# A hybrid layer on one core: a third pair of weight buffers while the mixers run, and the low parts of 27 weight units made by ScalarE and an accumulating DMA

## The chip, the cores and the metric

The kernel runs on one core of one Trainium2 chip. The time is the device time of one execution in microseconds (us). Each engine of the core works through its own list of instructions in order: TensorE (PE; its weight loads are listed as PEld), VectorE (DVE), ScalarE (ACT), GpSimd (POOL) and SyncE (SP). SP and POOL, and now and then ACT, also issue DMAs. A change of time of about 1% is what a measurement of this kernel can tell from no change.

## The reference, cut to what matters

One layer works on x of 512 x 1024 in float32. Its input is normalised, multiplied by one wide weight, and split among four sequence mixers (gated delta rule, RG-LRU, S5, RWKV-7) and four gates; the branches are merged, projected, and followed by an MLP and a last norm:

```python
h = _rmsnorm(x, norm1_g)
proj = h @ w_in                                   # 1024 x 6920: mixers' columns, then 4 x 1024 gate columns
p_gdn, p_lru, p_s5, p_rwkv, p_gate = _split(proj, (GDN_COLS, LRU_COLS, S5_COLS, RWKV_COLS, GATE_COLS))
ys = (_gdn_mixer(p_gdn, ...), _rglru_mixer(p_lru, ...), _s5_mixer(p_s5, ...), _rwkv7_mixer(p_rwkv, ...))
for i in range(N_BRANCH):
    term = sigmoid(gate_logits[:, :, i]) * (ys[i] @ w_branch[i])
    merged = term if merged is None else merged + term
x = x + merged @ w_out
x = x + square(relu(_rmsnorm(x, norm2_g) @ mlp_w1)) @ mlp_w2
return _rmsnorm(x, final_norm_g)
```

## The kernel before

Every large product is done in split precision. A weight comes in blocks of 128 x 1024 float32 (512 KB), called units here; there are 134 loads of them. For a unit u, `load` (L307) lets SP fetch the block into a buffer of the ring `raw` (four buffers, tags raw0 to raw3, taken in turn). `unit` (L316) then makes two parts of it: the high part `hi` is the block rounded to TensorE's short float32 form, written by ScalarE as a plain copy (`act`, L117), and the low part `lo` is what is left, block minus `hi`, written by VectorE (`tt`, L120). `gemm` (L337) issues for each of eight slices k three matmuls of 128 x 512: `hi` with the high part of x, `hi` with its low part, and `lo` with its high part, 24 in all. So the third matmul of a unit is the first that reads `lo`.

The pairs of `hi` and `lo` are two (DEEP = 2, tags hi0/lo0 and hi1/lo1) up to the MLP. The MLP takes two more tiles (`third`), so that three pairs take turns there; it also sums some of its weights with DMAs that add to what lies in the buffer (`accum_op=ADD`, issued by GpSimd, L330 and L332). Eighteen of these write a tile of the region c, six a raw buffer.

The work before the MLP is cut into steps named in PLAN: the first norm, the projection of each mixer's columns (two columns of weight units at a time), the mixers' own recurrences with many small matmuls, and the gates and branches between them. A scheduler turns the program into one fixed list for each engine; `priority(100 * u - 30000)` in `unit` places each unit's load and split ahead of most other work, as far as its buffers are free. So which instruction stands behind which on an engine is settled before the kernel runs, and an instruction that waits holds up all that stands behind it on that engine. The units 3 to 29 that are spoken of below are those of the last RWKV columns, S5, the delta rule, RG-LRU, and the first gate columns; unit 29 is done about a quarter of the way through the span.

Some names in the lists: acc is a unit's result in PSUM, zpr, t1pr and z3pr belong to one mixer's small products, glu to S5's last step, bkT and ktT to transposes for the recurrences, scrr and scu to scratch in HBM, c0, c1a, c1b, c2, c3 to regions of SBUF that many small tiles share (printed as c, c1a, c1b in the trace).

Of the kernel before, what the change touches and what calls it, by code (L numbers as in the profile page):

```python
# [9 lines left out]
F = mybir.dt.float32  # L10
R = mybir.dt.float32r
ACT = mybir.ActivationFunctionType
# [3 lines left out]
ADD, SUB, MUL, MAX = ALU.add, ALU.subtract, ALU.mult, ALU.max  # L16
# [40 lines left out]
GRAN = 32  # L57
DEEP = 2
NRAW = 4

GROUPS = ((8, True), (8, True), (8, True), (8, False))
REST = 21568
# [38 lines left out]
def trunk(ctx, tc, order, xT, wall, w8, prm, big, cst, gfr, out):  # L101
    nc = tc.nc
    V, A, G, P = nc.vector, nc.scalar, nc.gpsimd, nc.tensor

    const = ctx.enter_context(tc.tile_pool(name="const", bufs=1))
    wp = ctx.enter_context(tc.tile_pool(name="wp", bufs=1))
# [9 lines left out]
    def act(o, i, f, scale=1.0, bias=0.0):  # L116
        A.activation(out=o, in_=i, func=f, scale=scale, bias=bias)  # L117

    def tt(e, o, a, b, op):
        e.tensor_tensor(out=o, in0=a, in1=b, op=op)  # L120
# [72 lines left out]
    @contextmanager  # L193
    def priority(n):
        old = tc.cur_priority
        tc.cur_priority = n
        yield
        tc.cur_priority = old
# [32 lines left out]
    def v3(t, a):  # L231
        return t.rearrange("p (a b) -> p a b", a=a)
# [69 lines left out]
    third = []  # L302

    def place(key):
        if key not in order:
            order.append(key)
        return order.index(key)  # L307

    def load(key):
        n = count["raw"]  # L310
        count["raw"] += 1
        raw = wp.tile([128, 1024], F, tag=f"raw{n % NRAW}", name=f"raw{n}")
        nc.sync.dma_start(out=raw, in_=wall[place(key)])
        return raw

    def unit(key, more=None, chain=None):  # L316

        u = count["u"]
        count["u"] += 1
        with priority(100 * u - (30000 if u else 50000)):  # L320
            k = u % (DEEP + len(third) // 2)
            if k < DEEP:
                hi, lo = (wp.tile([128, 1024], R, tag=f"{e}{k}", name=f"{e}{u}") for e in ("hi", "lo"))
            else:
                hi, lo = third
            if chain is None:
                raw = load(key)
            else:
                raw = chain
                (G if more is None else nc.sync).dma_start(out=raw, in_=wall[place(key)], **({"accum_op": ADD} if more is None else {}))  # L330
            if more is not None:
                G.dma_start(out=raw, in_=wall[place(more)], accum_op=ADD)  # L332
            act(hi, raw, ACT.Copy)
            tt(V, lo, raw, hi.bitcast(F), SUB)
        return v3(hi, 8), v3(lo, 8)

    def gemm(o, w, rh, rl, nk=8, k0=0, first=True, last=True):  # L337
# [75 lines left out]
    def proj(col):  # L413

        o = pa("acc")
        gemm(o, unit(("in", col)), xgh, xgl)
        return o
# [964 lines left out]
    def branch(i, hf):  # L1382

        if i not in ysp:
            ysp[i] = split_y(ys[i], str(i))
        y = ysp[i]
        yh, yl = v3(y[0], 2), v3(y[1], 2)
        wh, wl = (t.rearrange("p (k m) c -> p k m c", k=2) for t in unit(("br", i, hf)))
        for mi, gt in enumerate(gates[i, hf]):
            m = 4 * hf + mi  # L1390
            o = pa("bacc")
            gemm(o, (wh[:, :, mi, :], wl[:, :, mi, :]), yh, yl, nk=2)
            if m not in mg:
                mg[m] = t2("mg", where=("c3",))
                tt(V, mg[m], o, gt, MUL)
            else:
                tt(V, gt, o, gt, MUL)
                tt(V, mg[m], mg[m], gt, ADD)
            fr(gt)
        gates.pop((i, hf))  # L1400
        if not any(k[0] == i for k in gates) and done_[i]:
            fr(*y)
        done_[i] = True
# [3 lines left out]
    def merge():  # L1407
        mh_, ml_ = t16("mh", R), t16("ml", R)
        mh, ml = v3(mh_, 8), v3(ml_, 8)
        for m in range(8):  # L1410
            act(mh[:, m, :], mg[m], ACT.Copy)
            tt(V, ml[:, m, :], mg[m], mh[:, m, :].bitcast(F), SUB)
            fr(mg[m])
        for m in range(8):
            o = pa("oacc")
            gemm(o, unit(("out", m)), mh, ml)
            tt(V, x2[m], o, x2[m], ADD)
        fr(mh_, ml_)
# [401 lines left out]
```

## Time and profile before

| | |
|---|---|
| median of three runs (lowest, highest) | 888.55 us (887.16, 894.03) |
| the profiled execution: time, span | 892.66 us, 890.9 us |
| PE busy, share of the span | 869.9 us, 98% |
| DVE, ACT, POOL busy | 549.8, 422.7, 24.2 us |
| mean granted clock of TensorE | 0.985 |

The profiled execution is 4.11 us above the median of the three. An engine's busy time counts its own instructions, not the issue of DMAs. Rows of groups give a line, an engine, an operation, the tile written and the tiles read, the count, the busy time and the mean of one, and then the idle time before them and what ended it. A row of a timeline gives the start, the duration, the engine (SPq for the issue of a DMA by SP), the line and the tiles. A row of windows gives a stretch of the span, the busy time of PE, PEld, DVE, ACT and POOL with their counts of instructions, the granted clock of TensorE, the busy share of the sixteen DMA engines and what they moved.

### The profile page before, as it was taken

Reading aid. Unit: us, or ns where it says so; the run is one execution under the profiler, and the core shown is the slowest. Engines: PE = TensorE matmul, PEld = TensorE weight load, DVE = VectorE, ACT = ScalarE, POOL = GpSimd, SP = SyncE. Lnnn points to the kernel's source line nnn. Section 1 sums busy time; section 2 is a strip of 40 time slices with the busy share of each in tenths; the row PEclk is TensorE's granted clock in tenths of the full one; section 3 lists DMA queues with packets and bytes.
Section 4 is the critical chain, followed back from the end, with each engine's and each line's share of the span. In section 5 each row is a group of like instructions: output and inputs, shape, how many; then the busy total and the mean of one; then the engine's idle time right before and its main releaser. Section 6 shows DMA issues by size and latency. Waiting matters only on the chain.

```text
span 890.9 us, 12990 instructions
## 1 busy us (share of the span) xinstructions
PE 869.9 (98%) x5175; PEld 696.8 (78%) x5175; DVE 549.8 (62%) x967; ACT 422.7 (47%) x584; POOL 24.2 (3%) x37
## 2 busy tenths in 40 slices
PE   8999999989899999999999999999999999999996
PEld 6777777768677777777888878888888888888885
DVE  6899796983666245845566554346436554868543
ACT  8735548845422243242633343756545443644533
POOL 1000000000000000000000000000100010010000
PEclk9999999998999889999999999999999999999999
DMA  8433344464355543243322223554775867563302
GB/s 292 134 117 103 113 118 93 108 175 112 119 177 149 155 121 94 95 128 109 106 96 95 94 94 121 187 143 166 145 207 146 259 161 196 162 146 113 118 24 95
DMA packets 79292, 119.96 MB, mean 135 GB/s; under 512 B 42544, under 2 KB 49392, under 8 KB 79216
## 3 DMA queue, kind: packets, MB, share of 16 engines
q1 hardware_dynamic: 51968, 100.40, 35.2%
q0 software_dynamic: 3456, 12.58, 8.3%
q10 hardware_dynamic: 23808, 6.16, 3.2%
q8 instruction: 40, 0.66, 0.3%
q14 instruction: 20, 0.16, 0.1%
HBM read 103.79 MB, written 13.17 MB: 131 GB/s over the span
## 4 chain that ended last, share of the span: by engine, by line
PE 85%; DVE 6%; ACT 3%; DMA 3%; issue 1%; ACTq 1%; SPq 0%; DVEq 0%
PE acc L114 28%; PE facc L114 20%; PE dacc L114 17%; PE oacc L114 5%; PE bacc L114 5%; DVE c L120 2%; PE oT L114 2%; DMA c1a<-gscr 1%; ACT c L117 1%; PE s L114 1%; DVE lo L120 1%; DVE c L129 1%; PE glu L114 1%; ACT L117 1%; PE gj L114 0%
## 5 line engine op out<-in xcount | busy, mean ns | idle before, releaser
L114 PE MATMUL acc<-c,hi 128*128 128x512 f32 x864 | 279.5, 401 | 4.4 <-DVE c L129 2.5
L117 ACT ACTIVATE hi<-raw 128x1024 fp32r<-128x1024 f32 x113 | 119.5, 1058 | 235.4 <-PE facc L114 73.6
L120 DVE TENSOR_TENSOR lo<-raw,hi 128x1024 fp32r<-128x1024 f32 x113 | 138.0, 1222 | 114.7 <-ACT hi L117 111.7
L114 PEld LDWEIGHTS acc<-c,hi 128*128 128x128 f32 x864 | 162.3, 190 | 45.3 <-DVE c L129 5.0
L114 PE MATMUL acc<-c,lo 128*128 128x512 f32 x432 | 174.9, 406 | 1.2 <-DVE lo L120 1.2
L114 PE MATMUL facc<-c,hi 128*128 128x512 f32 x336 | 103.4, 389 | 0.0
L114 PEld LDWEIGHTS acc<-c,lo 128*128 128x128 f32 x432 | 82.3, 191 | 21.1 <-DVE lo L120 2.8
L114 PEld LDWEIGHTS facc<-c,hi 128*128 128x128 f32 x336 | 63.1, 188 | 13.1
L117 ACT ACTIVATE c<-c 128x512 f32<-128x512 f32 (+5 forms) x101 | 63.8, 637 | 17.9 <-DVE c L120 11.1
L120 DVE TENSOR_TENSOR c<-c 128x16 f32<-128x16 f32 (+8 forms) x125 | 65.2, 536 | 6.9 <-ACT c L117 6.4
L114 PE MATMUL facc<-c,lo 128*128 128x512 f32 x168 | 65.6, 390 | 0.0
L114 PE MATMUL facc<-c,c1a 128*128 128x512 f32 x264 | 62.8, 391 | 0.0
L114 PE MATMUL dacc<-hi,c 128*128 128x512 f32 x176 | 57.4, 389 | 0.0
L114 PEld LDWEIGHTS facc<-c,c1a 128*128 128x128 f32 x264 | 49.3, 188 | 10.2
L117 ACT ACT_TABLE_LOAD x41 | 52.6, 1283 | 9.4 <-DMA c<-scu 3.1
L120 DVE TENSOR_TENSOR c1a<-raw,c1a 128x1024 fp32r<-128x1024 f32 x21 | 25.7, 1224 | 32.7 <-ACT c1a L117 32.6
L120 DVE TENSOR_TENSOR c<-acc,c 128x512 f32<-128x512 f32 x33 | 22.6, 689 | 37.0 <-PE acc L114 36.3
L114 PE MATMUL bacc<-c1a,hi 128*128 128x512 f32 x128 | 42.2, 413 | 0.0
L114 PE MATMUL oacc<-c,hi 128*128 128x512 f32 x128 | 39.8, 392 | 0.1
L117 ACT ACTIVATE c1a<-raw 128x1024 fp32r<-128x1024 f32 x21 | 22.2, 1058 | 36.5 <-PE facc L114 29.0
L114 PEld LDWEIGHTS dacc<-hi,c 128*128 128x128 f32 x176 | 33.0, 188 | 6.8
L114 PEld LDWEIGHTS facc<-c,lo 128*128 128x128 f32 x168 | 31.5, 188 | 6.5
(389 smaller groups left out, 1209.6 us busy)
## 6 DMA issues: line engine op xcount, KB each, us to landing
raw<-in_wall_dram SPq DMA_DIRECT2D x134, 512.0 KB, 3.5
c<-in_wall_dram POOLq DMA_DIRECT2D x18, 512.0 KB, 5.8
c<-in_wall_dram SPq DMA_DIRECT2D x6, 512.0 KB, 3.4
raw<-in_wall_dram POOLq DMA_DIRECT2D x6, 512.0 KB, 7.2
scg<-c1b SPq DMA_DIRECT2D x11, 256.0 KB, 2.3
c<-scg SPq DMA_DIRECT2D x11, 256.0 KB, 3.6
c1b<-in_xT_dram SPq DMA_DIRECT2D x8, 256.0 KB, 5.3
c<-in_xT_dram SPq DMA_DIRECT2D x8, 256.0 KB, 4.0
```

The costliest lines, as they stand in the source:

```text
L114: P.matmul(out=o, lhsT=l, rhs=r, start=start, stop=stop)
L117: A.activation(out=o, in_=i, func=f, scale=scale, bias=bias)
L120: e.tensor_tensor(out=o, in0=a, in1=b, op=op)
L129: V.scalar_tensor_tensor(out=o, in0=a, scalar=s, in1=b, op0=op0, op1=op1)
```

## The change

While the mixers run, the ring of raw buffers has two places in place of four. The two that come free become a third pair, named raw2 (high) and raw3 (low), which every third unit takes (u % 3 == 2). For units 3 to 29 VectorE no longer makes the low part: ScalarE writes the negative of `hi` into `lo`, and then a DMA issued by GpSimd reads the unit's block from HBM a second time and adds it to `lo`. In the MLP nothing changes but line numbers.

```diff
--- before.py
+++ after.py
@@ -58,6 +58,8 @@
 DEEP = 2
 NRAW = 4
 
+BYDMA = 3, 30
+
 GROUPS = ((8, True), (8, True), (8, True), (8, False))
 REST = 21568
 LV = {
@@ -309,7 +311,7 @@
     def load(key):
         n = count["raw"]
         count["raw"] += 1
-        raw = wp.tile([128, 1024], F, tag=f"raw{n % NRAW}", name=f"raw{n}")
+        raw = wp.tile([128, 1024], F, tag=f"raw{n % (NRAW if third else 2)}", name=f"raw{n}")
         nc.sync.dma_start(out=raw, in_=wall[place(key)])
         return raw
 
@@ -318,11 +320,13 @@
         u = count["u"]
         count["u"] += 1
         with priority(100 * u - (30000 if u else 50000)):
-            k = u % (DEEP + len(third) // 2)
-            if k < DEEP:
+            k = u % 3
+            if k < 2:
                 hi, lo = (wp.tile([128, 1024], R, tag=f"{e}{k}", name=f"{e}{u}") for e in ("hi", "lo"))
+            elif third:
+                hi, lo = third
             else:
-                hi, lo = third
+                hi, lo = (wp.tile([128, 1024], R, tag=t, name=f"{t}_{u}") for t in ("raw2", "raw3"))
             if chain is None:
                 raw = load(key)
             else:
@@ -331,7 +335,11 @@
             if more is not None:
                 G.dma_start(out=raw, in_=wall[place(more)], accum_op=ADD)
             act(hi, raw, ACT.Copy)
-            tt(V, lo, raw, hi.bitcast(F), SUB)
+            if BYDMA[0] <= u < BYDMA[1]:
+                act(lo, hi.bitcast(F), ACT.Copy, -1.0)
+                G.dma_start(out=lo, in_=wall[place(key)], accum_op=ADD)
+            else:
+                tt(V, lo, raw, hi.bitcast(F), SUB)
         return v3(hi, 8), v3(lo, 8)
 
     def gemm(o, w, rh, rl, nk=8, k0=0, first=True, last=True):
```

The lists of three engines show what it moves. First SP at the program's start: before, the blocks of the units 0 to 4 are fetched ahead of the constants (the rows from raw2 on).

```order
L254 DMA pr_81<-in_prm_dram 128x139
L313 DMA raw2_268<-in_wall_dram 128x1024
L313 DMA raw3_323<-in_wall_dram 128x1024
L313 DMA raw4_366<-in_wall_dram 128x1024
L255 DMA w8t_82<-in_w8_dram 128x64
L432 DMA scrr0_165<-c2_78 128x260 x4
L432 DMA scrr1_170<-c2_78 128x260 x4
```

After the change raw2 is followed at once by w8t, the eight scrr and the constants; the last of these, with the next weight blocks, read:

```order
L282 DMA c1a_76<-in_big_dram 128x256
L275 DMA c3_79<-in_cst_dram 128x128
L275 DMA c2_78<-in_cst_dram 128x64 x2
L282 DMA c2_78<-in_big_dram 128x256
L315 DMA raw3_323<-in_wall_dram 128x1024
L282 DMA c2_78<-in_big_dram 128x256
L315 DMA raw4_367<-in_wall_dram 128x1024
L315 DMA raw5_426<-in_wall_dram 128x1024
L315 DMA raw6_482<-in_wall_dram 128x1024
```

The block of unit 3 has moved behind all but one of these constants and that of unit 4 behind all of them, since their places in the ring are those of units 1 and 2.

Then ACT about two thirds of the way through the mixers. Before, from the high part of unit 19 to that of unit 20:

```order
L117 ACTIVATE hi19_1361<-raw19_1363 128x1024
L659 COPY c3_79<-bkT_1507 128x4x128
L659 COPY c3_79<-bkT_1513 128x4x128
L117 ACT_TABLE_LOAD
L117 ACTIVATE c3_79<-c3_79 128x512
L117 ACT_TABLE_LOAD
L117 ACTIVATE c1b_77<-c1b_77 128x512
L117 ACTIVATE hi20_2307<-raw20_2309 128x1024
```

After the change, from the high part of unit 19 to that of the next unit that is split, 21:

```order
L119 ACTIVATE hi19_1377<-raw19_1379 128x1024
L667 COPY c3_79<-bkT_1512 128x4x128
L667 COPY c3_79<-bkT_1518 128x4x128
L119 ACT_TABLE_LOAD
L119 ACTIVATE c3_79<-c3_79 128x512
L119 ACTIVATE lo19_1378<-hi19_1377 128x1024
L119 ACT_TABLE_LOAD
L119 ACTIVATE c1b_77<-c1b_77,cl_1041 128x512
L119 ACT_TABLE_LOAD
L119 ACTIVATE c3_79<-c1a_76 128x512
L119 ACTIVATE hi21_2360<-raw21_2362 128x1024
```

The negative of unit 19's high part (lo19) is new, three table loads stand in the row, and unit 21 comes ahead of unit 20.

Last, PE at the same place. Before, from the end of unit 19 to the start of unit 20:

```order
L114 MATMUL acc_1360<-c0_75,lo19_1362 128x512
L816 MATMUL ktT_1893<-cs_80,c3_79 128x128 x2
L816 MATMUL ktT_1897<-cs_80,c3_79 128x128 x2
L114 MATMUL acc_2306<-c0_75,hi20_2307 128x512 x2
L114 MATMUL acc_2306<-c0_75,lo20_2308 128x512
```

After, from the start of unit 19, whose matmuls go on after the first of unit 21:

```order
L116 MATMUL acc_1376<-c0_75,hi19_1377 128x512 x2
L666 MATMUL bkT_1524<-cs_80,c2_78 128x128 x4
L666 MATMUL bkT_1530<-cs_80,c2_78 128x128 x4
L116 MATMUL acc_1205<-c0_75,raw2_17_1206 128x512
L116 MATMUL acc_1205<-c0_75,raw3_17_1207 128x512
L116 MATMUL acc_2359<-c0_75,hi21_2360 128x512 x2
L824 MATMUL ktT_1910<-cs_80,c3_79 128x128 x2
L116 MATMUL acc_1376<-c0_75,lo19_1378 128x512
```

Unit 21's first matmuls have moved into the start of unit 19, between the end of unit 17 and the first matmul that reads lo19.

## The prediction

> **What bounds the kernel now.** I read the page first, then windows, the chain and PE's waits. The page's first part and the chain of waits:
>
> ```profile
> PE 869.9 (98%) x5175; PEld 696.8 (78%) x5175; DVE 549.8 (62%) x967; ACT 422.7 (47%) x584; POOL 24.2 (3%) x37
> ...
> PE 85%; DVE 6%; ACT 3%; DMA 3%; issue 1%; ACTq 1%; SPq 0%; DVEq 0%
> ```
>
> TensorE is busy 98% of the span and 85% of the chain. The change must be priced by what it does to TensorE's gaps, not by what it takes off VectorE. Three windows show where gaps are: the stretch of the converted units, the tail of the mixers, the rest.
>
> ```profile
> 22.00:172.00 150.00, 147.95 (x769) 113.65 (x768) 132.47 (x384) 91.46 (x123) 0.32 (x1) 1.00 0.41 112
> ...
> 172.00:250.00 78.00, 72.79 (x802) 57.19 (x802) 50.91 (x86) 38.59 (x51) 0.13 (x1) 0.93 0.52 143
> ...
> 350.00:891.00 541.00, 532.17 (x2484) 435.52 (x2482) 300.63 (x354) 243.38 (x326) 20.87 (x24) 1.00 0.46 132
> ```
>
> From 22 to 172 us PE already works 147.95 of 150 us at full clock, so at most 2.05 us can be won there, although VectorE is busy 132.47. From 172 to 250 PE lacks 5.21 us and the clock is 0.93. From 350 on lie mostly MLP units, which the change leaves as they are: nothing there. PE's waits by releaser name the gaps:
>
> ```profile
> PE t1pr L114 <- issue: 2.6, 1, 2.6
> ...
> PE glu L114 <- ACT c L117: 2.3, 1, 2.3
> PE acc L114 <- DVE lo L120: 1.2, 2, 1.0
> PE zpr L114 <- DMA c<-scrr: 0.9, 1, 0.9
> ```
>
> Only 1.2 us of PE's waiting is for a low part, in two waits. The other three, 5.8 us together, end steps of the mixers. A stretch of half clock, one of four whose windows read 0.50 (6.83, 3.40, 6.80 and 6.80 us long, 23.83 us in all):
>
> ```profile
> 199.05:205.88 6.83, 5.11 (x33) 4.29 (x33) 0.83 (x2) 1.45 (x4) 0.00 (x0) 0.50 0.63 156
> ```
>
> **The change part by part.** The prices of the pieces, from the groups and the DMA views (min, median and max of landing for L332 are those of accumulating DMAs alone):
>
> ```profile
> L117 ACT ACTIVATE hi<-raw 128x1024 fp32r<-128x1024 f32 x113 | 119.5, 1058 | 235.4 <-PE facc L114 73.6
> L120 DVE TENSOR_TENSOR lo<-raw,hi 128x1024 fp32r<-128x1024 f32 x113 | 138.0, 1222 | 114.7 <-ACT hi L117 111.7
> ...
> L117 ACT ACT_TABLE_LOAD x41 | 52.6, 1283 | 9.4 <-DMA c<-scu 3.1
> ...
> q1 hardware_dynamic: 51968, 100.40, 35.2%
> q0 software_dynamic: 3456, 12.58, 8.3%
> ...
> raw<-in_wall_dram SPq DMA_DIRECT2D x134, 512.0 KB, 3.5
> ...
> L332 POOL DMA_DIRECT2D raw<-in_wall_dram x6: 862/862/865, 585.1 to 754.5; - x6
> ...
> DMA to landing us min/median/max: 5.6/6.9/8.5
> ```
>
> *Throughput.* Removed: 27 subtractions of 1.22 us, 33 us of VectorE, worth nothing by themselves since PE lacks 2.05 us there. Added: 27 negatives on ScalarE, at the copy's 1.06 us 28.6 us; with 91.46 of 150 us busy it has room. Added: 27 accumulating DMAs. Queue q0 holds the 24 existing ones: 8.3% of 890.9 us over 24 is 3.1 us of all sixteen engines each, against 35.2% x 890.9 / 100.40 MB x 0.524 = 1.6 us for a plain block. Some 20 of them fall into the stretch 22 to 172, 62 us on 150, and lift its share from 0.41 to about 0.82: no bound by itself.
>
> *The steady course.* A unit is 24 matmuls. Three take 0.68 us (next rows: low-part matmuls at 30.38 and 31.06), so a unit takes 5.45 us and three pairs come round in 16.35. A pair is held for high part 1.06, negative 1.06, landing 5.8 (near the low end of L332, as loads of the stretch are sparser than in the MLP) and matmuls 5.45: 13.4 us. So 3.0 us of lateness is hidden, and the DMA costs nothing while ScalarE comes to the high part and to its negative in time. Where it does not, PE waits, and with the ring at two places a block can no longer be fetched four ahead. I look for the two places where this fails.
>
> *Start, unit 3.* SP's issues before, then PE at unit 3:
>
> ```profile
> 8.25 1.73 SPq L313 DMA_DIRECT2D raw<-in_wall_dram  x3
> ...
> 19.58 0.33 SPq L273 DMA_DIRECT2D c<-in_cst_dram  x1
> 20.91 2.01 SPq L280 DMA_DIRECT2D c<-in_big_dram  x3
> ...
> 24.45 0.38 SPq L313 DMA_DIRECT2D raw<-in_wall_dram  x1
> ...
> 29.93 0.62 PE L114 MATMUL acc<-c,hi 128*128 128x512 f32 x2
> 30.38 0.39 PE L114 MATMUL acc<-c,lo 128*128 128x512 f32 x1
> ...
> 31.06 0.39 PE L114 MATMUL acc<-c,lo 128*128 128x512 f32 x1
> ```
>
> Unit 3's block was among the loads at 8.25. By the order it now stands where unit 5's stood, at 24.45, and two constants (2 x 0.43) later; the two loads gone from the front give back 2 x 0.58. So it is issued at 24.2 to 25.3. Then landing 3.5, high part 1.06, negative 1.06, accumulating DMA 5.8: the low part is there at 35.6 or later. PE starts unit 3 at 29.93 and, with unit 4's two first matmuls pulled in, needs it 4 x 0.23 later, at 30.8. Wait 4.8. Ends: 3.6, if SP's pause of 1.0 before 20.91 goes too; 8.6, with issue at 25.3 and landing 8.5. I take **5**. Behind the waiting high part on ScalarE stand the copy of the norm's statistics and the RWKV steps, a second lateness inside these ends. POOL has nothing else queued there. By the Trainium skill (DMA: Bandwidth & Descriptors, section "Anatomy of one DMA") such a DMA costs about 2.0 us and the bytes over 436 GB/s, an estimate of 3.2 us for 512 KB; the wait would be 2 to 3 us shorter and the sum below near 10.5. Row L332's least, 5.6, disagrees, and I go by the row.
>
> *Unit 21.* ScalarE and PE before, at unit 19:
>
> ```profile
> 156.13 1.49 ACT L117 ACTIVATE c1b<-c1b,cl 128x512 f32<-128x512 f32 x2
> ...
> 158.04 1.04 ACT L117 ACTIVATE hi<-raw 128x1024 fp32r<-128x1024 f32 x1
> 158.99 1.05 ACT L659 COPY c<-bkT 128x512 f32<-128x512 f32 x2
> ...
> 161.35 0.63 ACT L117 ACTIVATE c<-c 128x512 f32<-128x512 f32 x1
> ...
> 153.80 1.14 PE L658 MATMUL bkT<-cs,c 128*128 128x128 f32 x8
> ...
> 161.19 0.50 PE L114 MATMUL acc<-c,lo 128*128 128x512 f32 x1 [1.00 <-DVE lo L120]
> ```
>
> By the new order ScalarE has, from the end of unit 19's high part to that of unit 21's: two copies 1.05, three table loads 3.85, three activations of 0.63 to 0.75 together 2.0, the negative 1.06, the high part 1.06: 9.0 us. PE has between the two only four matmuls (0.91) and eight transposes (1.14): 2.05. If unit 19's high part is just in time, as it was before (ready 159.08, and its low part late by 1.00), PE waits 7.0; if ScalarE is 7 us ahead, nothing. Neither is shown; I take the middle, **3.5**, ends 0 and 7. The block is no part of it: its place is free when unit 19's high part is made, and 0.4 to issue and 3.5 to land lie beside those 9.0 us.
>
> *The rest.* Other units where foreign work stands between high part and negative: for unit 19 that work is 1.05 + 1.28 + 0.63 = 3.0 us, all of the cover. I put **1.5**, ends 0 and 3, for such waits. The three mixers' waits (5.8 us) hang on round trips through HBM scratch that now share the queues with about twice the traffic, and on ScalarE with 1.06 us more per unit: **+2**, between -5.8 (PE's lateness at units 3 and 21 absorbs them) and +4 (each a little over half again as long). A half-clock stretch of 3.4 to 6.8 us costs half its length; the two new gaps of PE may bring one or two: **+2.5**, ends 0 and 6.8. The waits for VectorE's low part go: **-1.2**. The trace has no row for these last three, hence the wide ends.
>
> Sum: 5 + 3.5 + 1.5 + 2 + 2.5 - 1.2 = **13.3 us**. The profiled execution took 892.66, 4.11 above the median of its runs; on its own time 906.0, on the median of 888.55 **902**. The ends add up to -3.4 (3.6 - 5.8 - 1.2) and +28.2 (8.6 + 7 + 3 + 4 + 6.8 - 1.2), so 885 to 917.
>
> **The rivals.**
>
> *Faster: the relief of VectorE decides.* VectorE is 88% busy in 22 to 172 and some mixer steps queue on it; 33 us less there may bring them earlier, so that the waits of 7.0 us above (t1pr, glu, lo, zpr) shrink and the half-clock stretches that follow such gaps go (up to 23.83 / 2 = 11.9). At half of both: -9.5, **879**. It decides from the point where the starts at units 3 and 21 cost under 5 us together. For it: VectorE's load; against: only 1.2 us of PE's wait names VectorE's low part, and ScalarE, which takes the work, releases glu.
>
> *No difference.* The third pair's 3.0 us and a lead of ScalarE hide units 21 and the rest, and unit 3's 5 us are absorbed by the start of the mixers' chains: 5 - 1.2 to 0, **888 to 892**. For it: PE's bound; the MLP already runs on such DMAs with PE full and the sixteen engines at 0.98:
>
> ```profile
> 648.00:657.00 9.00, 9.00 (x42) 7.44 (x41) 3.25 (x3) 5.36 (x7) 1.73 (x2) 1.00 0.98 235
> ```
>
> Against: there the low part is made without a DMA behind it, and the block is known far ahead.
>
> *Much slower: the accumulating DMAs are late throughout.* With 8.5 landing and ScalarE 3.0 late a pair is held 1.06 + 3.0 + 1.06 + 8.5 + 5.45 = 19.1 us against 16.35, 0.9 us lost per unit, 24 us over 27, in place of the 5 us for unit 21 and the rest: 13.3 - 5 + 24 = 32, **921**. For it: a unit now asks 4.7 us of the sixteen engines in 5.45. Against: the window just shown. The Trainium skill (SBUF — State Buffer, section "SBUF: two separate sides") gives another cause: the descriptors of a DMA issued by GpSimd wait while VectorE runs an operation that takes both port pairs. By it these DMAs, beside a VectorE 88% busy, would be late as here; that the existing ones were all issued in about 0.86 us speaks against much of it, so it adds little to this rival's chance.
>
> **How the numbers follow.** My case has 0.53, the relief 0.13, no difference 0.22, much slower 0.12. About 1% (8.9 us, so 879.7 and 897.4) is what can be told from no change. Of my case a quarter lies below 897.4 (its lower end to 8.9 above the median), 0.13. Faster: 0.10 of the relief's 0.13. Same: 0.22 + 0.13 + 0.03 = 0.38. Slower: 0.40 + 0.12 = 0.52. The range takes in my case and no difference, down to 884 and up to 917; left out are most of the relief and of the last rival.
>
> **What would show it.** Right: PE waits for a DMA that writes lo near 31 us, 3.6 to 8.6 long; for a high part near 160, up to 7; 27 GpSimd DMAs landing in 5.6 to 6.9; 86 subtractions in place of 113; the DMA share of 22 to 172 near 0.8; nothing moved after 350 but the start. Wrong: no wait for a DMA above 1 us in the first 250 us, the clock near 1.00 in 172 to 250, or PE waiting on VectorE's steps less than now by several us. Landings at 8 us and waits in most of the 27 units would be the last rival.

## The result, and the profile after

The changed kernel takes 911.91 us (908.35 to 914.84) against 888.59, the median of the kernel before with a fourth run added: a ratio of 1.0253, 95% interval 1.0203 to 1.0302. It is slower, by 23.3 us between the medians. The profiled execution took 912.86 us with a span of 911.1, 20.2 us more than the span before, and the account below is made on the spans.

The page of the changed kernel, busy time and chain of waits:

```profile
PE 873.3 (96%) x5175; PEld 699.3 (77%) x5175; DVE 522.6 (57%) x940; ACT 447.9 (49%) x610; POOL 47.6 (5%) x64
...
PE 70%; DMA 9%; issue 8%; DVE 6%; ACT 5%; POOL 1%; ACTq 1%; SPq 0%; DVEq 0%; POOLq 0%
```

VectorE gave back 27.2 us (549.8 to 522.6) and ScalarE took 25.2, much as counted, but PE now fills 70% of the chain in place of 85%, and DMAs 9% in place of 3%. PE's busy time grew by 3.4 us, so 16.8 of the 20.2 us are new idle time. PE's waits after the change (total, times, longest):

```profile
PE acc L116 <- DMA lo<-in_wall_dram: 8.2, 3, 6.8
PE s5y L116 <- DMA c<-c1a: 6.8, 1, 6.8
PE acc L116 <- ACT hi L119: 5.1, 1, 5.1
...
PE us L116 <- ACT c1b L119: 2.0, 1, 2.0
PE s L116 <- ACT c L627: 1.7, 1, 1.7
```

The low part of one unit cost 6.8 us, the high part of another 5.1, and the first product of S5's last step waited 6.8 us for a DMA, at a place that had no wait before. The same two stretches as before:

```profile
22.00:172.00 150.00, 139.74 (x704) 104.36 (x703) 106.75 (x329) 90.21 (x118) 14.32 (x17) 0.98 0.69 155
172.00:250.00 78.00, 64.97 (x734) 53.29 (x734) 43.21 (x105) 47.62 (x64) 7.03 (x9) 0.80 0.69 164
```

PE works 139.74 us in the first where it worked 147.95, and 64.97 in the second where it worked 72.79 at a clock of 0.93. The stretches of half clock now lie at the three long waits (windows laid on them):

```profile
34.60:41.45 6.85, 4.09 (x10) 3.22 (x11) 4.54 (x28) 3.84 (x5) 0.86 (x1) 0.51 1.00 222
178.00:184.80 6.80, 4.79 (x12) 3.79 (x13) 3.92 (x15) 6.77 (x13) 0.86 (x1) 0.50 0.90 203
205.30:229.20 23.90, 17.13 (x164) 14.95 (x154) 8.49 (x16) 9.70 (x15) 0.86 (x1) 0.50 0.70 161
```

They hold 26.0 us of PE's work. Matmuls of 128x512 start about 0.43 us apart in them (38 to 41 us) against 0.23 at full clock, so they cost about half of that, 13.0 us; the four stretches before held 21.75, or 10.9. So the clock costs 2.1 us more. Idle 16.8, clock 2.1 and 1.3 left over make the 20.2.

### The profile page after: what moved, and what is told of

Same layout as the page of the kernel before. It is cut to its first block, busy times and chain, and to the rows that moved or that the text cites. A ratio compares the mean times of both kernels' runs of the same rounds, so it can differ in the third digit from the quotient of the medians.

```text
span 911.1 us, 13068 instructions
## 1 busy us (share of the span) xinstructions
PE 873.3 (96%) x5175; PEld 699.3 (77%) x5175; DVE 522.6 (57%) x940; ACT 447.9 (49%) x610; POOL 47.6 (5%) x64
## 4 chain that ended last, share of the span: by engine, by line
PE 70%; DMA 9%; issue 8%; DVE 6%; ACT 5%; POOL 1%; ACTq 1%; SPq 0%; DVEq 0%; POOLq 0%
PE facc L116 19%; PE acc L116 17%; PE dacc L116 16%; PE bacc L116 5%; PE oacc L116 5%; DMA lo<-in_wall_dram 2%; DMA c1a<-scrg 2%; ACT L119 2%; DVE c L122 2%; DVE c1a L122 1%; PE s5y L116 1%; ACT c L119 1%; DMA c<-c1a 1%; PE oT L116 1%; DVE c L131 1%
## 5 line engine op out<-in xcount | busy, mean ns | idle before, releaser
L116 PE MATMUL acc<-c,hi 128*128 128x512 f32 x576 | 191.2, 409 | 8.8 <-ACT hi L119 5.1
L119 ACT ACTIVATE hi<-raw 128x1024 fp32r<-128x1024 f32 x90 | 95.2, 1058 | 177.3 <-PE facc L116 68.2
L122 DVE TENSOR_TENSOR lo<-raw,hi 128x1024 fp32r<-128x1024 f32 x72 | 88.1, 1224 | 100.3 <-ACT hi L119 94.4
L116 PEld LDWEIGHTS acc<-c,hi 128*128 128x128 f32 x576 | 110.6, 194 | 38.9 <-ACT hi L119 5.9
L116 PE MATMUL acc<-c,lo 128*128 128x512 f32 x288 | 118.0, 410 | 8.2 <-DMA lo<-in_wall_dram 8.2
L116 PE MATMUL acc<-c,raw 128*128 128x512 f32 x432 | 109.0, 398 | 0.0
L116 PEld LDWEIGHTS acc<-c,raw 128*128 128x128 f32 x432 | 79.1, 188 | 18.6 <-issue 2.4
L119 ACT ACTIVATE c<-c 128x512 f32<-128x512 f32 (+4 forms) x101 | 63.8, 638 | 25.6 <-DVE c L122 15.3
L116 PEld LDWEIGHTS acc<-c,lo 128*128 128x128 f32 x288 | 55.7, 194 | 21.5 <-DMA lo<-in_wall_dram 9.4
L119 ACT ACTIVATE raw<-raw 128x1024 fp32r<-128x1024 f32 x32 | 33.8, 1056 | 31.3 <-PE acc L116 11.4
```

What stands on the lines that cost most here:

```text
L116: P.matmul(out=o, lhsT=l, rhs=r, start=start, stop=stop)
```

## The experiments

Two theories went into the first runs. A: the loss comes from the low parts being late or from the traffic of the accumulating DMAs. B: it comes from the ring cut to two places. Every edit of the program makes the scheduler write the lists anew, so a run compares two lists and not only two costs, unless the text says that the lists are the same.

**The third pair alone.**

```diff
-BYDMA = 3, 30
+BYDMA = 0, 0
```

> The third pair and the ring of two stay, but no unit's low part is made by a DMA: VectorE subtracts for all, as before the change. Theory A (the loss is the accumulating DMAs' lateness and traffic): back near the kernel before, 885 to 895 us, no wait of PE for a DMA into lo, the wait of s5y under 2 us. Rival B (the ring of two, which stops SP's fetches early, is the loss): 900 to 912 us, with PE waiting for high parts.

893.91 us, ratio 1.0061 (1.0040 to 1.0083): 5 us over the kernel before and 18 under the changed one. There is no wait for a DMA into lo, nor of s5y. B falls as the main cause: with VectorE subtracting for all units 18 of the 23 us are back. The third pair and the short ring bought nothing: PE worked 146.06 us of 22 to 172, against 147.95.

**The DMA alone, with two pairs and a ring of four.**

```diff
+BYDMA = 3, 30
...
-            tt(V, lo, raw, hi.bitcast(F), SUB)
+            if BYDMA[0] <= u < BYDMA[1]:
+                act(lo, hi.bitcast(F), ACT.Copy, -1.0)
+                G.dma_start(out=lo, in_=wall[place(key)], accum_op=ADD)
+            else:
+                tt(V, lo, raw, hi.bitcast(F), SUB)
```

> Two pairs and a ring of four as before the change, but the low parts of units 3 to 29 by ScalarE's negative and the accumulating DMA. A pair is then held for about 1.06 + 1.06 + 5.8 + 5.45 = 13.4 us against 10.9 us of two units, so theory A expects some 1.25 us lost per unit, 30 us or more over 27 units: 915 to 935 us, with PE's wait for DMAs into lo above 25 us. Rival B expects it faster than the changed kernel (912), since the fetches run four ahead: 890 to 900 us.

921.49 us, ratio 1.0409 (1.0334 to 1.0484). PE's waits:

```profile
PE acc L116 <- DMA lo<-in_wall_dram: 22.0, 9, 4.9
```

With two pairs nine waits and 22.0 us come from the low parts; the changed kernel has three and 8.2. So the third pair does hide most of the DMA's time, as the cover reckoned in the prediction says (2.5 us short per pair with two pairs, 3.0 to spare with three). The wait was expected above 25 us; rival B's 890 to 900 us is out here too. In sum PE idles as long in both profiled executions (37.2 and 37.8 us), since the long waits of s5y and for a high part are gone here. The longer time is half clock: its stretches hold 51.0 us of PE's work in place of 26.0.

**The same work off PE's path.** The kernel before, with the negative and the accumulating DMA added into one scratch tile.

```diff
+BYDMA = 3, 30
...
             tt(V, lo, raw, hi.bitcast(F), SUB)
+            if BYDMA[0] <= u < BYDMA[1]:
+                sh = wp.tile([128, 1024], R, tag="sh", name=f"sh{u}")
+                act(sh, hi.bitcast(F), ACT.Copy, -1.0)
+                G.dma_start(out=sh, in_=wall[place(key)], accum_op=ADD)
```

> The kernel before, unchanged in what PE reads, with 27 negatives on ScalarE and 27 accumulating DMAs added for units 3 to 29 into a tile that nobody reads. It prices ScalarE's extra work and the DMA traffic alone, since PE never waits for one of these DMAs. Theory A1 (about a third of the loss is traffic: the wait of s5y and the half clock behind it): 893 to 902 us, S5's transfers into its state tile landing in 6 to 8 us in place of 3.5. Theory A2 (all the loss is the lateness of low and high parts): 887 to 892 us.

908.57 us, ratio 1.0239 (1.0198 to 1.0280): far more than either version allowed, though PE reads none of it. The groups of this run show why it cannot be read as a price of traffic:

```profile
L119 ACT ACTIVATE sh<-hi 128x1024 fp32r<-128x1024 f32 x27 | 28.5, 1056 | 41.4 <-DMA sh<-in_wall_dram 37.4
```

ScalarE stood 37.4 us in front of the one scratch tile until its last DMA had landed, and all that is behind it in its list stood too. The run was badly built for its question: ScalarE's stalls, which lie between 50 and 253 us, and the traffic cannot be told apart in it.

**Only ScalarE's part.** The same without the DMA, so that nothing holds the scratch tile.

```diff
                 act(sh, hi.bitcast(F), ACT.Copy, -1.0)
-                G.dma_start(out=sh, in_=wall[place(key)], accum_op=ADD)
```

> The kernel before with 27 negatives of 128 x 1024 on ScalarE (28.6 us of work) into a tile nobody reads and no DMA. Theory T: 886 to 893 us, since ScalarE had room. If ScalarE's load on the mixers' chains is a cause of its own: 895 us or more, with PE's waits for ScalarE's c tiles grown by 5 us.

896.64 us, ratio 1.0070 (1.0028 to 1.0112), above what was expected if ScalarE had room. PE's longest wait in it:

```profile
PE acc L116 <- ACT hi L119: 6.4, 2, 5.6
```

So with 27 negatives alone, in the lists written for them, one high part is 5.6 us late, near 166 us. ScalarE had idle time in sum but not at that place.

**Only the DMAs.** Three runs, released by a small copy of the low part so that ScalarE does nothing more: accumulating, plain, and accumulating 4 KB in place of 480.

```diff
...
+                V.tensor_copy(out=tiny, in_=lo.bitcast(F)[:, 0:8])
+                G.tensor_copy(out=sh[:, 0:8], in_=tiny)
+                G.dma_start(out=sh, in_=wall[place(key)][:, 0:960], accum_op=ADD)
```

> The kernel before, PE reading what it read, with 27 accumulating DMAs of 480 KB added for units 3 to 29 into a tile nobody reads; no negative on ScalarE. Each is released by a copy of 8 columns of the unit's low part (0.17 us on VectorE), so it starts about when the real one does, and only GpSimd waits for the one before it. Theory T (the traffic lengthens the DMA round trips of the mixers): 897 to 908 us, with S5's or RWKV's transfers landing at 6 us and more. Theory S (the shadow run's 20 us came from ScalarE, which stood 37 us behind the one scratch tile): 887 to 894 us.

> The same program in the same order, with the 27 DMAs plain instead of accumulating. By the queues of the kernel before an accumulating DMA takes 3.1 us of the sixteen engines and a plain block 1.6. Theory T: about half of the loss of the accumulating ones, 892 to 899 us. Theory S: as the accumulating run, 887 to 894 us.

> The same edit with DMAs of 128 x 8 numbers (4 KB each) in place of 480 KB: what the new order of the lists, the small copies and the issue cost without the bytes. Both theories: 886 to 893 us; above 895 the new order itself would be a cause that neither names.

918.89, 912.96 and 916.91 us, ratios 1.0337 (1.0289 to 1.0385), 1.0253 (1.0206 to 1.0300) and 1.0297 (1.0242 to 1.0352). The 4 KB DMAs cost as much as the 480 KB ones, so neither theory explains these runs. Two things that the 4 KB run has as well make up all but 3 to 5 us of the longer spans. The tail of the mixers fell into one long stretch of half clock in all three, here in the run with 4 KB:

```profile
202.90:230.20 27.30, 24.88 (x218) 22.51 (x218) 7.81 (x16) 7.87 (x13) 1.05 (x2) 0.50 0.33 70
```

Half of 24.88 us is 12.4, in a stretch where the sixteen engines were busy only a third of the time. And TensorE ran slower in all three, in the MLP too, which the edit does not touch: 600 to 700 us in the run with 4 KB and in the kernel before:

```profile
600.00:700.00 100.00, 100.00 (x437) 81.74 (x436) 43.44 (x37) 53.26 (x71) 8.67 (x10) 1.00 0.65 168
```

```profile
600.00:700.00 100.00, 100.00 (x442) 82.79 (x442) 53.90 (x49) 55.50 (x71) 6.91 (x8) 1.00 0.64 180
```

PE's busy time less the cost of half clock is 859.0 us before and 857 to 862 in the changed kernel and the other runs, but 871 to 872 in these three. These runs therefore do not price the traffic. Between the accumulating and the plain one every list is the same, and 6 us lie between them; but half clock cost 21.2 us in the first and 13.9 in the second, so these 6 us are no price of the adding either.

**Was it the place in SBUF?** The three runs had moved the big region by 4032 bytes. The kernel before, with every list the same, and the region moved by 64 bytes:

```diff
+    wp.tile([128, 16], F, tag="pad", name="pad")
     count = {"u": 0, "raw": 0}
```

> The kernel before with 64 bytes per partition set aside ahead of the big region of SBUF; every engine's list is the same as before, row for row. In the three traffic runs TensorE was about 2% slower in the MLP too (434 to 438 matmuls per 100 us against 442), and their scratch tiles had moved that region by 4032 bytes. If the place is the cause (odd multiple of 64): 895 to 903 us with 434 to 438 matmuls in 600 to 700 us. If not: 886 to 892 us and 442.

891.77 us, ratio 1.0032 (1.0009 to 1.0056), and 443 matmuls in 600 to 700. A shift by 64 bytes does not do it; the shift by 4032 bytes itself was not tried alone, and what made TensorE 2% slower in those three runs stays open.

**Where in the 27 units the loss lies.** Two runs of the changed kernel with the DMA for fewer units.

```diff
-BYDMA = 3, 30
+BYDMA = 3, 18
```

> The changed kernel with the DMA only for units 3 to 17; VectorE subtracts for 18 and up. Theory A: the start (6.8 us of wait, 3.4 of half clock) stays, the late high part of unit 21 and the wait of s5y go: 897 to 903 us. If the loss were spread evenly over the 27 units: 888.6 + 15/27 x 23 = 901 us, but then the waits for DMAs into lo would be in most units; the waits tell the two apart, not the time.

904.89 us, ratio 1.0189 (1.0154 to 1.0225), 2 us above theory A's range. Its waits for low parts are two, one of 6.5 us at the start:

```profile
PE acc L116 <- DMA lo<-in_wall_dram: 6.9, 2, 6.5
PE acc L116 <- ACT hi L119: 4.4, 1, 4.4
```

The wait for a high part, unit 21's, did not go, against what was expected, though units from 18 up have VectorE's subtraction here. The wait of s5y went.

```diff
-BYDMA = 3, 30
+BYDMA = 6, 18
```

> The changed kernel with the DMA for units 6 to 17 only; VectorE subtracts for the others. Theory P (the loss sits at places: the start 6.8 us, unit 21 5.1 us, S5's transfer 6.8 us): 893 to 898 us, near the run with the third pair alone (893.9), and 7 to 10 us under the run with units 3 to 17 (904.9). Theory E (each such unit costs its share): 893.9 + 12/27 x 18 = 902 us, 2 us under units 3 to 17.

893.15 us, ratio 1.0064 (1.0040 to 1.0089): the same as the third pair alone, with twelve units through the DMA and no wait for a low part at all. The longest waits of PE:

```profile
PE b8T L1214 <- ACT c L1215: 3.6, 1, 3.6
PE acc L116 <- DVE c L131: 2.5, 6, 0.8
PE acc L116 <- ACT hi L119: 2.0, 1, 2.0
...
PE acc L116 <- ACT raw L119: 1.5, 1, 1.5
```

The last row is a high part too, of the third pair.

An even share per unit (902) is out: the loss sits at places. Giving units 3 to 5 to the DMA costs 11.7 us between these two runs (7 to 10 were expected), a wait of 6.5, the half clock behind it and what the later lists make of it; units 6 to 17 cost nothing. So the 23 us come in steps: 5 with the third pair and the short ring, none with units 6 to 17, 12 with units 3 to 5, and 7 (904.89 to 911.91) with units 18 to 29. Each step also has lists of its own.

**S5's transfer.** The changed kernel without the DMA for the units issued beside it.

```diff
-            if BYDMA[0] <= u < BYDMA[1]:
+            if BYDMA[0] <= u < BYDMA[1] and not 22 <= u <= 25:
```

> The changed kernel without the DMA for units 22 to 25, whose accumulating DMAs were issued at 194 to 208 us, beside the transfers of S5's states (issued 202.9 to 207.7, landing in 8.0 to 8.4 us against 3.4 to 5.3 before). Theory Q (their traffic is what makes these transfers land late): landing back to 3.5 to 5.5, the wait of s5y from 6.8 to 2 us or less, the time 904 to 908 us. If S5's scan on VectorE is what is late: the wait stays at 5 us or more and the time at 909 to 913 us.

The transfers landed in 4.8 to 5.7 us, about as theory Q has it:

```profile
PE s5y L116 <- DMA c<-c1a: 5.5, 1, 5.5
...
DMA to landing us min/median/max: 4.8/5.3/5.7
```

The wait fell only from 6.8 to 5.5, and the time is 912.49 us, ratio 1.0267 (1.0246 to 1.0289), no less than the changed kernel. So the traffic does lengthen the transfers, and the wait has a second part: S5's states come late to the transfer. Here the one that PE waits for was issued 1.9 us later than in the changed kernel (206.21 against 204.35), with VectorE's four subtractions back in its list, one of them in the chain that ends at s5y. The time says little about either part. PE idled 32.6 us in place of 37.8, but two late stretches of half clock, which the changed kernel does not have, hold 20.1 us of its work and cost 10.1:

```profile
306.10:316.30 10.20, 10.20 (x163) 8.45 (x164) 1.62 (x5) 1.64 (x4) 0.00 (x0) 0.50 0.53 175
323.20:333.30 10.10, 9.94 (x55) 7.71 (x56) 1.67 (x4) 1.72 (x5) 0.00 (x0) 0.50 0.39 128
```

**Plain in place of accumulating, every list the same.** The low part is then the block itself.

```diff
-                G.dma_start(out=lo, in_=wall[place(key)], accum_op=ADD)
+                G.dma_start(out=lo, in_=wall[place(key)].bitcast(R))
```

> The changed kernel, every list the same row for row, with the 27 DMAs plain instead of accumulating: the low part then holds the block itself and the subtraction is left out. It prices what the accumulating costs over a plain transfer at the same places. By the traffic runs (5.7 us to landing against 4.5) and the queues (3.1 us of the engines against 1.6): waits for DMAs into lo from 8.2 to 4 to 6 us, the wait of s5y from 6.8 to 3 to 5, the time 904 to 908 us. If the place in the chain is all that counts: 910 us and more.

904.13 us, ratio 1.0181 (1.0164 to 1.0198). PE's waits, and of the DMA issues the row of the low parts, with the median us to landing:

```profile
PE acc L116 <- DMA lo<-in_wall_dram: 6.0, 1, 6.0
PE s5y L116 <- DMA c<-c1a: 5.6, 1, 5.6
PE acc L116 <- ACT hi L119: 4.4, 1, 4.4
...
lo<-in_wall_dram POOLq DMA_DIRECT2D x18, 512.0 KB, 5.1
```

That the DMA adds is worth 7.8 us of the 23: landings of 7.3 against 5.1, one wait for a low part in place of three, all three long waits a little shorter. The three places stay, so two thirds of the loss stay when the DMA only copies. They hold all that is left of the change: the ring and the order of the lists (5 us with the third pair alone), the negatives, and a second transfer of any kind.

No version beat the kernel before; the nearest, the third pair alone and units 6 to 17, are both 0.6% over it.

## Why the prediction was right, and where its sizes were wrong

The direction and its reason held: PE was bound, VectorE's 27 us bought nothing, and time was lost where PE met a late part. The forecast of 902 us was 10 us low, inside the range; on the profiled executions 13.3 us were forecast and 20.2 came. Step by step, on the spans:

**The start, 5 us taken (3.6 to 8.6): 6.75.** The profile shows PE at unit 3:

```profile
37.36 0.79 PE L116 MATMUL acc<-c,lo 128*128 128x512 f32 x1 [6.75 <-DMA lo<-in_wall_dram]
```

The parts of the sum were off in opposite ways. SP issues, then GpSimd's:

```profile
21.59 0.38 SPq L315 DMA_DIRECT2D raw<-in_wall_dram  x1
```

```profile
28.75 1.00 POOL L340 DMA_DIRECT2D lo<-in_wall_dram  x1 [25.32 <-ACT lo L119]
```

The block was fetched at 21.59, not 24.2 to 25.3, since SP came through the rows ahead of it faster (the eight scrr took 5.20 us in place of 6.44, and pauses closed up). But the accumulating DMA, issued at 28.75, let PE go at 37.36, 8.6 us later where 5.8 was taken. Its kind, all 27 issues:

```profile
DMA to landing us min/median/max: 5.3/7.2/10.2
```

The value 5.8 was too near the low end; the argument that the stretch is sparser than the MLP was wrong, the sixteen engines being at 1.00 in 34.6 to 41.45 and at 0.69 in 22 to 172. The estimate of 3.2 us by the Trainium skill (DMA: Bandwidth & Descriptors, section "Anatomy of one DMA"), which the prediction set aside, is further off: no accumulating DMA landed under 5.3, and the plain ones of the last run took 3.6 to 7.4.

That the wait came so near to the middle of its ends is in part luck. The run without units 22 to 25 has the same lists up to 190 us; in its profiled execution the same DMA landed in 5.9 us, and the wait was half as long:

```profile
34.45 0.79 PE L116 MATMUL acc<-c,lo 128*128 128x512 f32 x1 [3.47 <-DMA lo<-in_wall_dram]
```

**Unit 21, 3.5 taken (0 to 7): 5.1.** ScalarE's and PE's rows at that place:

```profile
170.12 1.06 ACT L119 ACTIVATE hi<-raw 128x1024 fp32r<-128x1024 f32 x1
...
178.91 1.04 ACT L119 ACTIVATE hi<-raw 128x1024 fp32r<-128x1024 f32 x1
...
180.01 1.22 PE L116 MATMUL acc<-c,hi 128*128 128x512 f32 x2 [5.14 <-ACT hi L119]
```

From the end of one high part to the end of the next are 8.77 us, reckoned as 9.0; ScalarE's lead was under 2 us rather than 3.5. A wait of this kind does not need the DMA at that unit: 4.4 us came at unit 21 with subtractions from unit 18 on, 3.5 in two waits with the DMA for units 6 to 17 alone, and 5.6 near 166 us with ScalarE's negatives alone.

**The steady course, nothing, and 1.5 for strays: 1.4.** Two further waits for low parts, 8.2 - 6.8. The three pairs' cover is confirmed by units 6 to 17. The DMA share of 22 to 172 came to 0.69, not 0.82.

**The mixers' waits, +2 taken (-5.8 to +4): +6.0. This is the step that failed.** The waits named before (t1pr, glu, zpr, with 0.7 for wT) were 6.5 us; now t1pr has 1.1, zpg 0.6 and b8T 0.3, 2.0 in all, so 4.5 were absorbed. But s5y (6.8), us (2.0) and s (1.7) appeared, which had no row in the list of waits before and so were not priced. S5's states go in four transfers, and s5y starts when the third has landed. Before, the third:

```profile
195.97 0.63 SPq L1312 DMA_DIRECT2D c<-c1a  x1
...
DMA to landing us min/median/max: 3.6/3.6/3.6
```

It landed at 199.6, and PE's s5y began at 201.21: a slack of 1.6 us, and so no wait and no row. After the change the chain of waits runs to the same place like this (start, duration):

```profile
181.61 0.96 ACT lo L119
182.57 0.65 ACT c L667 x2
183.41 1.08 ACT raw L119
...
188.64 0.95 ACT raw L119
189.94 1.07 ACT c1b L119
191.03 1.22 DVE c L827
...
196.12 2.19 DVE c1a L1313 x2
...
204.35 8.32 DMA c<-c1a
212.76 1.08 PE s5y L116 x4
```

The row at 204.35 is the third transfer. It landed 13.1 us later than before (212.7 against 199.6): 8.4 for the later issue and 4.7 for the longer landing (8.3 us against 3.6). PE finished what stood ahead, the t1pr products, only 4.7 us later (205.78 against 201.07). The difference less the slack is the wait: 13.1 - 4.7 - 1.6 = 6.8. Beyond PE's own lateness the issue is thus 3.7 us late and the landing 4.7; in the run without units 22 to 25 these are 5.5 and 1.5, in the run with plain DMAs 3.4 and 3.8. So both parts count.

The landing grew with the traffic. Why the issue is late is only partly shown: from 167.67 to 191.03 the chain is on ScalarE, with three negatives in it (2.9 us), and VectorE's S5 scan comes behind it; the rest is work that was there before, in another order. With negatives alone, in yet another order, s5y waited 0.5 us. No run separates ScalarE's longer list from the order.

**The clock, +2.5: +2.1.** About right in sum, wrong in course: two of the old stretches, at 301 and 329, went, and one of 23.9 us came, which began among the small t1pr products 0.7 us before s5y's wait.

Together 6.75 + 5.1 + 1.4 + 6.0 + 2.1 - 1.2 = 20.2 (rounded), the difference of the spans. The waits in this sum are 1.3 us more than the 16.8 of new idle time, as smaller waits went; the 1.3 us of busy time left over above stand against that.

**The rivals.** The relief of VectorE did not decide: PE waits less for t1pr and glu, but three other waits took their place. No difference fails by its interval. Late throughout (921) fails too: waits for low parts are three in 27 units. The run with two pairs came to its time, with nine. Nor did VectorE hold the issues up: all 27 took 0.86 to 1.00 us.

## What to carry to other kernels

Where one engine is full, a cover in steady state is easy to reckon and was right here; the loss came where the order breaks it: the first units, whose loads had lost their places, and one place where foreign work stands between two steps of a unit on ScalarE. Before moving work onto an engine, look not only at PE's listed waits but at chains that land just in time: a wait of zero with little slack behind it (1.6 us here) has no row. If a DMA is to make an operand, take the upper end of its landings beside full queues, and leave out the first units.

## What was not expected of the hardware

A stretch of half clock can be long while TensorE works: 23.9 us with 17.13 busy in the changed kernel, 27.3 us with 24.88 busy in the run with 4 KB DMAs, both over the many small products of the mixers' tail. In the run with two pairs one is filled by PE's rows from end to end:

```profile
209.67:233.56 23.89, 23.89 (x209) 21.65 (x210) 11.26 (x20) 12.46 (x17) 0.86 (x1) 0.50 0.55 143
```

The Trainium skill (TensorE: Matmul & The Clock Gate, section "Part 1: The HAM clock gate") lets the clock come back after about 3.4 us of sustained work; here it stayed away for seven to eight times that, so work of this kind does not seem to count as such, which no run here isolates.

TensorE 2% slower over whole runs (434 to 438 matmuls in 100 us of the MLP in place of 442), in three programs whose MLP is that of the kernel before, is open.
